# Output projection of a two-sequence encoder layer as four pairs of seven products

## The chip, the cores and the metric

The kernel runs on one core of a Trainium2 chip. The metric is device time in microseconds (us) of one execution; smaller is better. The engines are called PE (TensorE), DVE (VectorE), ACT (ScalarE), POOL (GpSimd) and SP (SyncE, which issues most transfers).

## The reference, cut to what matters

The reference is one layer of an encoder over two sequences of 512 tokens and 1024 channels: an S5 scan, a differential attention and a cross attention over a memory, whose outputs are gated, projected up and added into `merged`; then an output projection, and a feed-forward network. All is float32.

```python
merged = None
for n in range(N_BRANCH):
    term = jax.nn.sigmoid(g[..., n * D_MODEL:(n + 1) * D_MODEL]) * (branches[n] @ p['w_up'][l, n])
    merged = term if merged is None else merged + term
x = x + merged @ p['w_out'][l]
xn2 = _rmsnorm(x, p['norm_ffn'][l])
gate, up = jnp.split(xn2 @ p['w_ffn_in'][l], 2, axis=-1)
return x + (jax.nn.silu(gate) * up) @ p['w_ffn_out'][l]
```

The change is at `merged @ p['w_out'][l]`: 1024 tokens (both sequences) by 1024 channels by 1024 channels.

## The kernel before

**Matmuls.** Activations lie with channels on the 128 partitions and the tokens of both sequences (2 x 512) along the free axis, in 8 tiles of 128 channels. Every float32 operand is split into a high and a low part (`split`, L134 and L135: ACT writes the high part as float32r, DVE subtracts it from the source for the low part), and each product is three matmuls of 128 x 128 by 128 x 512: high by high, high by low, low by high (`mm3`).

**Seven products.** The feed-forward network already multiplies 2 x 2 blocks with seven products instead of eight. The two blocks of tokens are the two sequences, the two blocks of K are channel tiles i and i + 4, and the two blocks of output channels are two tiles. `quad_sums` makes four sums and differences of a pair of activation tiles, `quad_split` splits the seven operands into a pair of slots `th` and `tl` (seven columns of 512 each), `weights4` makes the seven weight operands `A11`, `A12`, `A22`, `S1` to `S4` of two weight tiles (four sums by POOL, L1022 to L1025), and `quadrants` (L1101) adds the seven results into four blocks. `products` gives the order of the matmuls.

**The stages here.** `merge_units(1, ...)` is the last merge: eight units of 24 matmuls; DVE scales each result by the gate (L789), POOL adds it into `mg[m]` (L793), and then `split` makes `mgh[m]`, `mgl[m]`. The output projection follows: `out_tile(m, s, w)` issues, for output tile m and sequence s, 8 K steps of three matmuls; DVE adds the residual x (L960) into `x1[m]`, SP stores it to `x1D` in DRAM, and ACT and POOL collect the sum of squares for the norm (`sum_sq`, L181 and L182). The order of the tiles is 0, 4, 1, 5, 2, 6 and then 3 and 7 sequence by sequence. `operands(i)` scales `x1[i]` and `x1[i + 4]` by `norm_ffn` and makes the operands of the feed-forward network from them. Then the feed-forward loop runs 22 blocks of 84 matmuls (`products(i, w)`); the first, i = 0, takes its K steps so that the operands of pairs 2 and 3 are wanted last. The norm's factor is applied to the results, so only `rstd(accs[s])` in block 0 has to wait for the sums of squares.

**What sets the order.** The framework's scheduler orders the instructions of each engine at build time, by the order of the program where they are ready, and puts the semaphores in. A pool with n buffers hands them out in turn; a new tile waits until all accesses to the one n before it are done. `issue_after` puts instructions behind a given one of their engine, and `InOrder`, with `on` set, keeps one engine to the order of the program; before the change only PE has one. The rooms that matter: `wf`, `wh`, `wl` (weights, two buffers each), `ld` (four), `x1` (four), `th0`, `tl0`, `th1`, `tl1` (two each), six PSUM banks `mm` and two `tr` (`aux`).

Of the kernel before, what the change touches and what calls it, by code (L numbers as in the profile page):

```python
# [10 lines left out]
F32 = mybir.dt.float32  # L11
# [8 lines left out]
P = 128  # L20
# [33 lines left out]
class InOrder:  # L54
# [10 lines left out]
    def matmul(self, *args, **kw):  # L65
        return self.put(self.eng.matmul(*args, **kw))  # L66

    def transpose(self, *args, **kw):
        return self.put(self.eng.transpose(*args, **kw))  # L69
# [3 lines left out]
def encoder(ctx: ExitStack, tc: tile.TileContext, a, out):  # L73
    nc = tc.nc
    V, S, PO, PE = nc.vector, nc.scalar, nc.gpsimd, InOrder(tc, nc.tensor)
# [55 lines left out]
    def split(hi, lo, src, scale=None):  # L131

        if scale is None:
            h = S.copy(hi, src)  # L134
            l_ = V.tensor_tensor(out=lo, in0=src, in1=hi.bitcast(F32), op=ALU.subtract)  # L135
# [380 lines left out]
    with behind():  # L516

        mrs = cst.tile([P, 4], F32, name="mrs")
        mbc = cst.tile([P, L], F32, name="mbc")
# [249 lines left out]
    mgh, mgl = [None] * KD, [None] * KD  # L769

    def merge_in(n, tags="yyyy"):
        bh_ = [slot(tags[t], [P, NT], F32R, f"yh{t}") for t in range(4)]
        bl_ = [slot(tags[t], [P, NT], F32R, f"yl{t}") for t in range(4)]
# [6 lines left out]
    def merge_units(n, b, m, first=False, last=False):  # L780
# [11 lines left out]
        if not first:  # L792
            PO.tensor_tensor(out=mg[m], in0=mg[m], in1=gt, op=ALU.add)  # L793
# [5 lines left out]
    mes = ExitStack()  # L799
    b0 = []  # L800

    def first_in():
        b0.append(merge_in(0, ["qk", "qk", "qk", "v"]))
        yield 0

    def merges():
        res_.close()
        xp_es.close()
        open_tags(mes, side="right", mg=8, y=8)
# [119 lines left out]
    open_tags(phase, ms=16)  # L929
    ves = ExitStack()  # L930
    open_tags(ves, z=6)
    b1 = merge_in(1, "zzzy")
    for m in range(KD):
        for _ in merge_units(1, b1, m, last=True):
            pass

    mes.close()
    ves.close()
    tes = ExitStack()
    open_tags(tes, side="right", th0=2, tl0=2)
    aes = ExitStack()
    aps = aes.enter_context(tc.tile_pool(name="ffs", bufs=1, side="right", reuse_waits="tile"))
    ses = ExitStack()
    open_tags(ses, side="right", x1=4, xr=2, ts=1)
    x1D = drp.tile([KD, P, NT], F32, name="x1D")
    x1 = {}  # L950
    accs = [new_acc() for _ in range(NS)]

    def out_tile(m, s, w):
        cs = slice(s * L, (s + 1) * L)
        xr = slot("xr", [P, L], name="xr")
        nc.sync.dma_start(xr, a["xT"][s, :, m, :])
        ps = bank()
        for k in range(KD):
            mm3([ps], w[0], w[1], [(mgh[k][:, cs], mgl[k][:, cs])], k, KD)
        V.tensor_tensor(out=x1[m][:, cs], in0=ps, in1=xr, op=ALU.add)  # L960
        nc.sync.dma_start(x1D[m, :, cs], x1[m][:, cs])
        sum_sq(accs[s], x1[m][:, cs], m == 0)

    last_p = None

    def quad_sums(xa_, xb_, tag="ts", third=PO):
# [5 lines left out]
        last_p = third.tensor_tensor(out=t_[:, 2], in0=b22, in1=b12, op=ALU.subtract)  # L972
        V.tensor_tensor(out=t_[:, 1], in0=b22, in1=t_[:, 0], op=ALU.subtract)
        V.tensor_tensor(out=t_[:, 3], in0=b21, in1=t_[:, 1], op=ALU.subtract)
        return t_

    def quad_room(i):
        j = i // 2 % 2
        return slot(f"th{j}", [P, 7, L], F32R, "th"), slot(f"tl{j}", [P, 7, L], F32R, "tl")

    last_q = None

    def quad_split(i, xa_, xb_, t_):

        nonlocal last_q
# [3 lines left out]
        split(th[:, 3:5], tl[:, 3:5], t_[:, 0:2])  # L989
        last_q = split(th[:, 5:7], tl[:, 5:7], t_[:, 2:4])  # L990
        return th, tl

    def operands(i):

        xa_, xb_ = x1[i], x1[i + 4]
        S.activation(out=xa_, in_=xa_, func=AF.Copy, scale=vcol("norm_ffn", i))
        V.tensor_scalar_mul(xb_, xb_, vcol("norm_ffn", i + 4))
        return quad_split(i, xa_, xb_, quad_sums(xa_, xb_))

    H = 4 * P  # L1000

    def weights4(i):

        nonlocal last_w
        a1, a2 = (wp.tile([P, DM], F32, tag="wf", name="wf") for _ in range(2))
        nc.sync.dma_start(a1, a["w_fg"][i])
        last_w = nc.sync.dma_start(a2, a["w_fu"][i])
        res = {}

        def sp(pool, src, sfx, *names):  # L1010
            n = len(names) * H
            nonlocal last_s
            wh, wl = (pool.tile([P, DM], F32R, tag=t_ + sfx, name=t_, bufs=2) for t_ in ("wh", "wl"))
            last_s = split(wh[:, :n], wl[:, :n], src)
# [3 lines left out]
        sp(wp, a1, "", "A11", "A12")  # L1018
        sp(wp, a2[:, H:], "", "A22")
        yield res  # L1020
# [771 lines left out]
```

## Time and profile before

| | us |
|---|---|
| three runs, median | 1604.06 |
| three runs, lowest and highest | 1603.86, 1604.61 |
| profiled execution, span from first to last instruction | 1603.0 |
| PE busy in it | 1587.1 |
| DVE, ACT, POOL busy | 1162.9, 640.0, 541.6 |

The page gives no other time of the profiled execution than its span. Its mean granted clock is 0.997 of full speed. Lines of the profile name a source line (L66), an engine, an operation and the tiles written and read (`bkmm<-th,wh`: a PSUM bank from operands `th` and weights `wh`); a releaser is what ended an engine's wait. All PE instructions are recorded by a helper and have its lines (L66 matmul, L69 transpose), so they are told apart by their tiles. A matmul's own row is longer than the distance to the next one, since matmuls are pipelined.

### The profile page before, as it was taken

What the parts mean: (1) busy time and instruction counts of PE and PEld (TensorE: products, weight loads), DVE (VectorE), ACT (ScalarE), POOL (GpSimd) and SP (SyncE); (2) the same over time, 40 slices, a digit from 0 to 9 for tenths busy, and PEclk for the clock granted to TensorE, in tenths of its full rate; (3) what the DMA queues carried; (4) which work ended last, traced back from release to release, by engine and by line L of the source; (5) the groups of instructions that cost most, each with busy time, mean ns of one, the idle gap of its engine ahead of it and who ended that gap; (6) DMA issues with size and microseconds to landing.
All of it is one profiled execution on the core that took longest, in us unless ns stands there. A gap on an engine that the chain in (4) does not pass through costs nothing.

```text
span 1603.0 us, 21625 instructions
## 1 busy us (share of the span) xinstructions
PE 1587.1 (99%) x7838; PEld 1314.8 (82%) x7838; DVE 1162.9 (73%) x1856; ACT 640.0 (40%) x1142; POOL 541.6 (34%) x449
## 2 busy tenths in 40 slices
PE   9999999999999999999999999999999999999997
PEld 7888788888898778778878878888888888788877
DVE  7976996076773766776465678888898778988654
ACT  6544323274652455574133443332333323233323
POOL 0010100001333220300343367676665553444653
PEclk9999999999999999999999999999999999999998
DMA  9554523576762111244454432333323223986222
GB/s 366 173 160 150 179 95 125 180 273 201 252 224 102 54 47 40 73 156 140 145 190 132 144 118 80 131 119 129 121 106 118 79 88 119 344 332 198 80 66 106
DMA packets 104891, 237.86 MB, mean 148 GB/s; under 512 B 13520, under 2 KB 45008, under 8 KB 104784
## 3 DMA queue, kind: packets, MB, share of 16 engines
q1 hardware_dynamic: 104784, 236.47, 43.1%
q8 instruction: 62, 1.02, 0.3%
q14 instruction: 45, 0.37, 0.1%
HBM read 165.16 MB, written 71.27 MB: 147 GB/s over the span
## 4 chain that ended last, share of the span: by engine, by line
PE 87%; issue 4%; DVE 3%; DMA 3%; POOL 2%; ACT 0%; SPq 0%; POOLq 0%; DVEq 0%; ACTq 0%
PE bkmm L66 75%; PE bksc L66 3%; PE bktr L66 2%; PE bkoo L66 2%; PE bktr L69 2%; DVE tl L135 1%; PE bktr L1626 1%; POOL mg L793 1%; PE bktr L1597 1%; DMA yt<-bD 1%; PE bktr L1686 0%; PE bktr L1687 0%; PE bktr L1685 0%; PE bktr L1565 0%; DMA acc<-in_w_fo 0%
## 5 line engine op out<-in xcount | busy, mean ns | idle before, releaser
L66 PE MATMUL bkmm<-xh,wh 128*128 128x512 f32 x640 | 255.4, 399 | 0.0
L66 PE MATMUL bkmm<-xh,wl 128*128 128x512 f32 x640 | 250.9, 392 | 0.0
L66 PE MATMUL bkmm<-xl,wh 128*128 128x512 f32 x640 | 250.5, 391 | 0.0
L66 PE MATMUL bkmm<-tl,wh 128*128 128x512 f32 (+1 forms) x621 | 241.2, 388 | 1.4 <-DVE tl L135 1.4
L66 PE MATMUL bkmm<-th,wl 128*128 128x512 f32 (+1 forms) x621 | 241.0, 389 | 0.9 <-DVE wl L135 0.9
L66 PE MATMUL bkmm<-th,wh 128*128 128x512 f32 (+1 forms) x621 | 241.1, 389 | 0.0
L134 ACT CAST wh<-wf 128x1024 fp32r<-128x1024 f32 (+1 forms) x134 | 117.9, 880 | 224.1 <-PE bkmm L66 179.8
L135 DVE TENSOR_TENSOR wl<-wf,wh 128x1024 fp32r<-128x1024 f32 (+1 forms) x134 | 145.1, 1083 | 50.2 <-ACT wh L134 45.7
L66 PEld LDWEIGHTS bkmm<-xh,wh 128*128 128x128 f32 x640 | 120.3, 188 | 30.3 <-issue 7.9
L66 PE MATMUL bkmm<-th,w 128*128 128x512 f32 x432 | 141.5, 392 | 2.7 <-DVE up L1101 1.0
L66 PEld LDWEIGHTS bkmm<-xh,wl 128*128 128x128 f32 x640 | 120.2, 188 | 26.7 <-issue 1.3
L66 PEld LDWEIGHTS bkmm<-xl,wh 128*128 128x128 f32 x640 | 120.4, 188 | 22.4 <-issue 0.4
L66 PEld LDWEIGHTS bkmm<-tl,wh 128*128 128x128 f32 x621 | 116.6, 188 | 25.9 <-DVE tl L135 2.1
L66 PEld LDWEIGHTS bkmm<-th,wl 128*128 128x128 f32 x621 | 116.5, 188 | 25.7 <-DVE wl L135 1.7
L66 PEld LDWEIGHTS bkmm<-th,wh 128*128 128x128 f32 x621 | 116.6, 188 | 23.9
L1165 POOL TENSOR_TENSOR up<-up,acc 128x512 f32<-128x512 f32 x44 | 83.6, 1920 | 87.8 <-DVE up L1101 87.8
L454 POOL TENSOR_TENSOR raw<-raw 128x128 f32<-128x128 f32 x28 | 15.2, 545 | 284.4 <-DVE nb L545 206.5
L66 PEld LDWEIGHTS bkmm<-th,w 128*128 128x128 f32 x432 | 80.9, 188 | 23.8 <-DVE up L1101 3.4
L793 POOL TENSOR_TENSOR mg<-mg,gl 128x1024 f32<-128x1024 f32 x16 | 43.5, 2720 | 139.0 <-DVE gl L789 139.0
L548 ACT ACTIVATE e<-bksc,nb 128x512 f32<-128x512 f32 (+1 forms) x96 | 58.8, 615 | 73.5 <-DVE nb L543 51.9
L66 PE MATMUL bkmm<-tl,w 128*128 128x512 f32 x216 | 84.2, 390 | 0.0
L66 PE MATMUL bkmm<-yh,wh 128*128 128x512 f32 x192 | 75.9, 397 | 0.8 <-ACT wh L134 0.4
(641 smaller groups left out, 3527.8 us busy)
## 6 DMA issues: line engine op xcount, KB each, us to landing
wf<-in_w_in SPq DMA_DIRECT2D x40, 512.0 KB, 3.9
wD<-hl SPq DMA_DIRECT2D x28, 512.0 KB, 2.9
w<-wD SPq DMA_DIRECT2D x28, 512.0 KB, 5.0
gD<-gt SPq DMA_DIRECT2D x24, 512.0 KB, 2.8
gl<-gD SPq DMA_DIRECT2D x24, 512.0 KB, 3.4
wf<-in_w_fg SPq DMA_DIRECT2D x22, 512.0 KB, 3.7
wf<-in_w_fu SPq DMA_DIRECT2D x22, 512.0 KB, 3.6
aD<-ac SPq DMA_DIRECT2D x22, 512.0 KB, 3.1
```

What stands on the lines that cost most here:

```text
L66: return self.put(self.eng.matmul(*args, **kw))
L69: return self.put(self.eng.transpose(*args, **kw))
L134: h = S.copy(hi, src)
L135: l_ = V.tensor_tensor(out=lo, in0=src, in1=hi.bitcast(F32), op=ALU.subtract)
L454: PO.tensor_tensor(out=a22, in0=a21, in1=a22, op=ALU.add)
L548: last_x = S.activation(out=e, in_=sc, func=AF.Exp, bias=nb, scale=scale, accum_out=sm)
L793: PO.tensor_tensor(out=mg[m], in0=mg[m], in1=gt, op=ALU.add)
L1165: PO.tensor_tensor(out=up, in0=up, in1=accs[s], op=ALU.mult)
L1597: PE.matmul(kp[64 * hf : 64 * hf + 48, g * 144 : (g + 1) * 144], l_[:, 2 * hf + g, :], o_[:, 4 * g4 + 2 * hf + g, :], start=(l_ is lr48), ...
L1626: PE.matmul(ps[:, g * P : (g + 1) * P], w_[:, gg * P : (gg + 1) * P], u_[:, 8 * o + gg, :], start=True, stop=True)
```

## The change

The output projection takes the form of the feed-forward network. `mg[i]` and `mg[i + 4]` become the operands `mo[i]` of seven products (`quad_steps`, which makes the four differences in place, all on DVE), and output tiles m and m + 4 are made as a pair: `out_first` (pair 0, K step by K step over seven PSUM banks), `out_pair` (pairs 1 to 3, product by product in two or three banks that are read between products and written on; in pair 3 the last three products go K step by K step). The results are added into tiles that already hold x.

`split_by_transfer` is a second way to split: ACT writes the high part and then its negative as the low part, and a transfer issued by POOL adds the source to it. It is used for the second half of the operands `mo[0]` to `mo[2]` and of pairs 0 and 2 of the feed-forward network, for `A11`, `A12` and `A22` of all pairs, for `S1` to `S4` of pairs 1 to 3, and for all but `A22` of the feed-forward network's first block.

PE is kept in program order from pair 0 to the end of block 0, DVE, ACT and POOL from `early` to the end of the stage. `early`, called in the middle of pair 3, prepares block 0's weights and the operands of pairs 1 (read back from `x1D`) and 2; the four last additions of pair 3 stand behind it. Block 0 takes its products in a new order and all its matmuls come before those of `rstd`. Rooms: `th1`, `tl1` three, `th0`, `tl0` and `th2`, `tl2` one each, `sw` (two, for `S1` to `S4`, two inputs of the merge and later two tiles of the output). The columns of `th` and `tl` have another order, and `SEVEN` with them.

```diff
-    V, S, PO, PE = nc.vector, nc.scalar, nc.gpsimd, InOrder(tc, nc.tensor)
+    V, S, PO, PE = (InOrder(tc, e_) for e_ in (nc.vector, nc.scalar, nc.gpsimd, nc.tensor))
...
+    def split_by_transfer(hi, lo, src):
+        S.copy(hi, src)
+        n_ = S.activation(out=lo, in_=src, func=AF.Copy, scale=-1.0)
+        return n_, PO.dma_start(lo.bitcast(F32), src, accum_op=ALU.add)
...
-        if last:
-            mgh[m] = slot("ms", [P, NT], F32R, f"mgh{m}")
-            mgl[m] = slot("ms", [P, NT], F32R, f"mgl{m}")
-            split(mgh[m], mgl[m], mg[m])
...
+    def quad_steps(th, tl, xa_, xb_, far=False):
...
+        split(th[:, 0], tl[:, 0], b11)
+        split(flat(th[:, 1:3]), flat(tl[:, 1:3]), xb_)
+        V.tensor_tensor(out=b11, in0=b12, in1=b11, op=ALU.subtract)
+        last_p = V.tensor_tensor(out=b12, in0=b22, in1=b12, op=ALU.subtract)
+        V.tensor_tensor(out=b22, in0=b22, in1=b11, op=ALU.subtract)
+        V.tensor_tensor(out=b21, in0=b21, in1=b22, op=ALU.subtract)
+        yield th, tl
+        put = split_by_transfer if far else split
+        put(flat(th[:, 3:5]), flat(tl[:, 3:5]), xa_)
+        last_q = put(flat(th[:, 5:7]), flat(tl[:, 5:7]), xb_)
...
-    def out_tile(m, s, w):
...
-        for k in range(KD):
-            mm3([ps], w[0], w[1], [(mgh[k][:, cs], mgl[k][:, cs])], k, KD)
-        V.tensor_tensor(out=x1[m][:, cs], in0=ps, in1=xr, op=ALU.add)
...
+    SEVEN = (("A11", 0), ("S2", 6), ("A12", 1), ("S3", 4), ("S1", 3), ("A22", 5), ("S4", 2))
...
+    for i in range(4):
         for m in (i, i + 4):
...
+            for _ in merge_units(1, b1, m, third=V if m == KD - 1 else PO):
+                pass
+        if i < 3:
+            mo.append(quad_in_place(*room_of(1), mg[i], mg[i + 4], far=True))
...
+    mo.append(quad_in_place(*room_of(2), mg[3], mg[7]))
...
+    def out_first(m, w):
...
+        for j, k in ((0, 0), (0, 1), (1, 0), (1, 1), (0, 2), (1, 2), (0, 3), (1, 3)):
+            for nm, o in SEVEN:
+                if nm[0] == "AS"[j]:
+                    product(ps[nm], w[nm], o, mo, (k,))
...
+    def out_pair(m, w):
+        xa_, xb_ = x_in(m)
+        pu, pw, pv = bank(), bank(), bank()
+        product(pu, w["A11"], 0, mo)
+        product(pv, w["A12"], 1, mo)
+        plus(xa_[:, :L], pu)
+        plus(xa_[:, :L], pv)
+        product(pu, w["S2"], 6, mo, more=True)
+        product(pw, w["S1"], 3, mo)
+        plus(xa_[:, L:], pu)
+        if m < 3:
...
+        else:
+            plus(xa_[:, L:], pw)
+            plus(xb_[:, L:], pw)
+            p4, pl = bank(), bank()
+            for k in range(4):
+                product(pu, w["S3"], 4, mo, (k,), more=True)
+                product(p4, w["S4"], 2, mo, (k,))
+                product(pl, w["A22"], 5, mo, (k,))
+            w0.append(early())
+            plus(xb_[:, :L], pu)
+            plus(xb_[:, L:], pu)
+            plus(xa_[:, L:], p4)
+            plus(xb_[:, :L], pl)
...
+    def early():
+        for e_ in (V, S, PO):
+            e_.on = True
+        wg = weights4(a["w_fg"][0], a["w_fu"][0], ("A11", "S1", "S3"), True)
+        w_ = next(wg)
+        x2_ = [slot("ld", name="xo") for _ in range(2)]
+        for t_, r_ in zip((1, 5), x2_):
+            nc.sync.dma_start(r_, x1D[t_])
+        scaled_x(1, *x2_)
+        scaled_x(2, *xs_[2])
+        next(wg)
+        next(wg)
+        ops.append(quad_in_place(*quad_room(1), *x2_))
+        g = quad_steps(*quad_room(2), *xs_[2], far=True)
+        ops.append(next(g))
+        next(wg)
+        next(g, None)
+        return w_
...
+    for m in range(4):
+        w = all_of(weights4(a["w_out"][m], a["w_out"][m + 4], FAR if m else FAR[:2]))
+        xs_.append((out_pair if m else out_first)(m, w))
+        if m == 0:
+            ops.append(quad_in_place(*quad_room(0), *scaled_x(0, *xs_[0]), far=True))
+    ops.append(quad_in_place(*quad_room(3), *scaled_x(3, *xs_[3], *(slot("ld", name="xs") for _ in range(2)))))
+    x_sums(3, *xs_[3])
...
         if i == 0:
...
+            ps = [bank() for _ in range(6)] + [aux()]
+            ps = [ps[j] for j in (0, 2, 3, 4, 6, 1, 5)]
+            near_, far_ = ("A11", "S2", "A12", "S1"), ("A22", "S3", "S4")
+            for k, names in ((0, near_), (1, near_), (0, far_), (1, far_), (2, near_ + far_), (3, ("A11", "A12", "A22")),
+                             (3, ("S2", "S3", "S1", "S4"))):
+                for nm in names:
+                    j = [n_ for n_, _ in SEVEN].index(nm)
+                    product(ps[j], w[nm], SEVEN[j][1], ops, (k,))
```

In `weights4`, a split whose first name is in `moved` goes by `split_by_transfer`; `FAR` is `("A11", "A22", "S1", "S3")`.

More of the change, by code (lines that the diff above doesn't have):

```diff
@@ L993, in operands, with flat, room_of @@
[L993 to L998, printed above, removed]
+    open_tags(ves, z=1)
+    x1D = drp.tile([KD, P, NT], F32, name="x1D")
+    accs = [new_acc() for _ in range(NS)]
+    def flat(t_):
+        return t_.rearrange("p a n -> p (a n)")
+    def room_of(j):
+        return slot(f"th{j}", [P, 7, L], F32R, "th"), slot(f"tl{j}", [P, 7, L], F32R, "tl")
@@ new lines, in product @@
+    def product(ps, w, o, ops_, ks=range(4), more=False):
+        nonlocal last_mm
+        wh, wl = w
+        mark = {"skip_group_check": True} if more else {}
+        for k in ks:
+            th, tl = ops_[k]
+            ws_ = slice(k * P, (k + 1) * P)
+            PE.matmul(ps, wh[:, ws_], th[:, o], start=(k == 0 and not more), stop=False, **mark)
+            PE.matmul(ps, wh[:, ws_], tl[:, o], start=False, stop=False, **mark)
+            last_mm = PE.matmul(ps, wl[:, ws_], th[:, o], start=False, stop=(k == 3), **mark)
```

256 lines of the change are left out of this document (143 added, 113 removed).

## The prediction

> **What bounds the kernel now.** I read the page's table of engines first, then the chain of waits, then the stages around the change, then single rows.
>
> ```profile
> PE 1587.1 (99%) x7838; PEld 1314.8 (82%) x7838; DVE 1162.9 (73%) x1856; ACT 640.0 (40%) x1142; POOL 541.6 (34%) x449
> ...
> PE 87%; issue 4%; DVE 3%; DMA 3%; POOL 2%; ACT 0%; SPq 0%; POOLq 0%; DVEq 0%; ACTq 0%
> ```
>
> TensorE (PE) is busy all the time and carries the chain; the other engines only matter where they make it wait. The next rows are the stages of busy time (last merge; output projection; the start of the feed-forward loop, "FFN 0" below), one piece of the chain, and the two places in FFN 0 where PE stands.
>
> ```profile
> 812.00:855.20 43.20, 43.20 (x192) 35.74 (x192) 27.18 (x32) 11.62 (x14) 20.49 (x8) 1.00 0.48 164
> 855.20:942.40 87.20, 87.20 (x386) 72.23 (x385) 47.44 (x48) 33.46 (x39) 35.08 (x22) 1.00 0.49 148
> 942.40:965.00 22.60, 21.22 (x102) 17.15 (x101) 22.32 (x21) 13.92 (x19) 16.03 (x13) 1.00 0.32 97
> ...
> 811.79 130.82 PE bkmm L66 x576
> ...
> 957.88 0.49 PE L66 MATMUL bkmm<-th,wh 128*128 128x512 f32 x1
> 958.98 0.50 PE L66 MATMUL bkmm<-tl,wh 128*128 128x512 f32 x1 [0.60 <-DVE tl L135]
> ...
> 960.02 0.40 PE L66 MATMUL bkmm<-th,wl 128*128 128x512 f32 x1
> 961.20 0.50 PE L66 MATMUL bkmm<-tl,wh 128*128 128x512 f32 x1 [0.78 <-DVE tl L135]
> ```
>
> The columns after the window are its length, then PE, PEld, DVE (VectorE), ACT (ScalarE), POOL (GpSimd), the granted clock, the DMA share and GB/s. The clock is 1.00 throughout. The chain runs through merge and output projection as 576 matmuls without a hole in 130.82 us: one costs 130.82 / 576 = 0.227 us, not the 0.39 us of its own row, since matmuls overlap. FFN 0 starts without a gap and then stands twice: 958.98 - 957.88 - 0.227 = 0.87 us and 961.20 - 960.02 - 0.227 = 0.95 us, together 1.8 us, for low parts (`tl`) from VectorE. So time is won here only by issuing fewer matmuls, and lost wherever an operand comes later than PE's order wants it.
>
> **What it removes.** The output projection now issues 8 tiles x 2 sequences x 8 K steps x 3 = 384 matmuls; four pairs of seven products of 4 K steps x 3 are 336. 48 x 0.227 = 10.9 us of path. FFN 0 still has 84. The 1.8 us of standing in FFN 0 I count as removed and price that boundary afresh: the ceiling is 12.7 us.
>
> **What it adds**, in the rows that price it:
>
> ```profile
> L134 ACT CAST wh<-wf 128x1024 fp32r<-128x1024 f32 x8 | 8.4, 1054 | 17.8 <-PE bkmm L66 17.8
> L134 ACT CAST wh<-wf 128x512 fp32r<-128x512 f32 x1 | 0.6, 626 | 1.3 <-PE bkmm L66 1.3
> L996 ACT ACTIVATE x<-x,vec 128x1024 f32<-128x1024 f32 x4 | 4.6, 1154 | 8.1 <-DMA x1D<-x 8.1
> ...
> L135 DVE TENSOR_TENSOR wl<-ws,wh 128x1024 fp32r<-128x1024 f32 x2 | 2.5, 1226 | 6.4 <-ACT wh L134 6.4
> L971 DVE TENSOR_TENSOR ts<-x 128x512 f32<-128x512 f32 x3 | 2.1, 693 | 9.3 <-ACT x L996 9.3
> L960 DVE TENSOR_TENSOR x<-bkmm,xr 128x512 f32<-128x512 f32 x16 | 10.9, 684 | 17.3 <-PE bkmm L66 17.3
> L1022 POOL TENSOR_TENSOR ws<-wf 128x512 f32<-128x512 f32 x1 | 1.3, 1297 | 1.0 <-DMA wf<-in_w_fu 1.0
> ...
> aD<-ac SPq DMA_DIRECT2D x22, 512.0 KB, 3.1
> ...
> fb<-aD SPq DMA_DIRECT2D x9, 512.0 KB, 6.2
> ...
> x1D<-x SPq DMA_DIRECT2D x16, 256.0 KB, 2.4
> ```
>
> No row of before shows an accumulating transfer, nor any DMA that POOL issues. A plain 512 KB store out of SBUF lands in 3.1 us and a 256 KB one in 2.4 us; the slowest 512 KB row quoted is 6.2 us, and a POOL sum of 1.3 us can stand ahead of the issue. So a low part made this way comes 2.4 to 7.5 us after ScalarE's second pass, instead of 1.23 us after its first. I take 3.1 and 2.4, the rows nearest in kind (the source is SBUF, the queues about half empty at a DMA share of 0.49). Below nothing I do not go: a transfer that waits for a pass of ScalarE cannot land before it.
>
> [...]
>
> Steady state is covered. A pair is 84 x 0.227 = 19.1 us. Per pair ScalarE makes eight weight passes (six of 1.05 us, two of 0.63 us) and four squares, under 11 us; VectorE adds seven or eight results, 8 x 0.68 = 5.5 us; POOL does four sums and four additions to the squares, 8 x 1.3 = 10.4 us, and four issues. Room for `A11` comes free after 24 of 84 matmuls, so the next split has 60 x 0.227 = 13.6 us. In one PSUM bank reused by three products each reading has 12 matmuls, 2.7 us, for 0.68 us. SyncE's queue gets eight 512 KB loads of x for sixteen of 256 KB, eight stores for sixteen, and two loads back of pair 1: nothing at that DMA share. Three places are not covered: where one stage's weights or operands hand their room to the next.
>
> *Merge to pair 0.* `A22` takes the room of the last merge unit's weights, free 0.39 - 0.23 = 0.16 us after the merge. Two passes of 0.63 us and 2.4 us of transfer: 3.8 us. PE wants the low part as its ninth matmul, at 8 x 0.227 = 1.8 us. Cost 2.0 us. This hides `mo[3]`, whose last part is wanted only after 63 matmuls, 14.3 us.
>
> *Pair 0 to pair 1.* Pair 0 runs K by K, so the room of `A11`, `A12` comes free at its 69th matmul: 16 x 0.227 - 0.39 = 3.2 us before pair 1. Two passes of 1.05 us and 3.1 us: 2.0 us after the start; wanted at the third matmul, 0.45 us. Cost 1.5 us.
>
> *Pair 3 to FFN 0.* Count from the first FFN 0 matmul. VectorE, ScalarE and POOL are put in program order here, and `early()` stands ahead of pair 3's own last four additions, so those wait for it, and PE for them. ScalarE may begin when the room of `A11` is free, 61 x 0.227 - 0.39 = 13.5 us before. Two passes (2.1), four scalings (4.6) and two passes (2.1) bring it to -4.7. The operands of pair 1 may be made: `mo[0]` was free at -6.0, which is what the K order of the last pair is for. High part 0.63, low part 0.69: -3.4; the next high part is ready, and on VectorE follow 1.23, four differences 2.8 and two low parts 2.5: 3.3. Pair 1's last column is wanted at 15 matmuls, 3.4 us: just covered. Then pair 2's first half (0.69 + 1.23 + 2.8) and `A22` (0.69): 8.7; two additions from `pu`: 10.1. Instructions of VectorE follow one another closer than their rows:
>
> ```profile
> 936.07 1.23 DVE L135 TENSOR_TENSOR wl<-ws,wh 128x1024 fp32r<-128x1024 f32 x1 [1.67 <-ACT wh L134]
> 937.22 0.69 DVE L960 TENSOR_TENSOR x<-bkmm,xr 128x512 f32<-128x512 f32 x1
> ```
>
> by 0.08 us, so 14 of them take 1.1 us less: 9.0. PE wants that bank after 24 matmuls, 5.4 us: it stands 3.6 us. Pair 3's operands come after the additions: two scalings, high parts, then 1.23 + 2.8 + 2.5 us on VectorE, ending near 20.3, for a column wanted 45 matmuls after the bank, 9.0 + 10.2 = 19.2, plus one for the low part: 1.0 us more. Cost 4.6 us. The two norm factors (`rstd`) go from the middle of FFN 0 to its end; the matmuls of the next block are free of the fixed order and cover them.
>
> The sum: -12.7 + 2.0 + 1.5 + 4.6 = -4.6 us. The profiled span of 1603.0 us becomes 1598.4 us. The median of the runs, 1604.06 us, is 1.1 us above that span, so I forecast **1599.5 us**.
>
> **The rivals.** *The transfers land late (slower).* Place: the low parts of `A22`, `A11` and of pair 2's differences. At 7 us instead of 3.1 us (6.2 us and something ahead of it on POOL) the first two boundaries lose 3.9 us each; pair 2's last part, whose second pass ends at 10.9, lands at 17.9 for a want at 9.0 + 18 x 0.227 + 0.9 = 14.0, and 3.9 us minus the 1.0 us it absorbs are lost: 10.7 us more, 1610 us. It decides from about 5 us: there the two boundaries lose 3.8 and pair 2 0.9, and the gain is gone. For it: nothing of this kind has been seen here, and loads under load take 6.2 us. Against it: plain stores in the same stage are at 2.4 us.
>
> *VectorE becomes the bound in the last merge.* The differences of three pairs move into a stage where POOL adds too.
>
> ```profile
> L793 POOL TENSOR_TENSOR mg<-mg,gl 128x1024 f32<-128x1024 f32 x15 | 41.1, 2742 | 42.7 <-DVE gl L789 42.7
> ...
> L135 DVE TENSOR_TENSOR mgl<-mg,mgh 128x1024 fp32r<-128x1024 f32 x8 | 12.9, 1619 | 11.7 <-ACT mgh L134 11.7
> ...
> 947.95 1.78 DVE L135 TENSOR_TENSOR tl<-x,th 128x512 fp32r<-128x512 f32 x1
> ...
> 952.68 2.32 DVE L135 TENSOR_TENSOR tl<-x,th 128x1024 fp32r<-128x1024 f32 x1
> ```
>
> An addition of two SBUF operands takes 0.69 us alone and 1.78 us beside POOL; of 1024 columns 1.23 and 2.32. VectorE was busy 27.2 of 43.2 us here, 12.9 of them `mgl`, which goes. Three pairs' work is 3 x (0.69 + 1.23 + 4 x 0.69) = 14.0 us alone, 28.3 in all, which fits; wholly beside POOL it is 3 x (1.78 + 2.32 + 4 x 1.78) = 33.7, 48.0 in all, 4.8 us too much, and pair 0's two low parts that VectorE still makes come 2.2 us later: 7.0 us, 1606.5 us. It decides where a pair's work passes (43.2 - 14.3) / 3 = 9.6 us. The POOL additions fill 7 x 2.7 us = 19 us of the 43.2, so half overlap is likelier, and that fits. [...]
>
> *All covers hold.* The transfers land within 2 us and the scheduler finds `early()` earlier; about 1.5 us of stalls are left: 1593 us. Against it stands the fixed order on VectorE, which is counted out above.
>
> That matmuls do not fall by 48 I exclude: the loops give the count.
>
> **How the numbers follow.** This kernel can be told from no change at about 0.2%, 3.2 us. My forecast has a chance of 0.42 (its own range 1596 to 1603.5, of which 0.30 is more than 3.2 us under the median and 0.12 within it); late transfers 0.26 (0.24 slower, 0.02 within); VectorE 0.20 (0.14 slower, 0.06 within); covers hold 0.12. Faster 0.42, same 0.20, slower 0.38. Both signs hold much of the chance, so the range goes from just above the best case, 1594, to the late transfers, 1611.
>
> **What would show it.** PE matmuls down by 48 to 7790. In the groups, PE's idle time put down to a DMA or `wl` near the ninth matmul of pair 0 and the third of pair 1 (about 2.0 and 1.5 us), and to the additions of pair 3 in FFN 0 (about 3.6 us). The DMA table should show the accumulating transfers with their time to land: 3 us confirms, over 5 us is the first rival. VectorE's mean for the differences in the merge tells the second: near 0.7 us or near 1.8 us, and whether weights of merge units come late. I am wrong if PE stands more than 12.7 us longer than before between the merge and the end of FFN 0, or if stages away from it change by more than 1 us.

## The result, and the profile after

The changed kernel takes 1653.71 us in the median of four runs (1650.86 to 1655.55), the kernel before 1604.09 on the same chip: a ratio of 1.0309, 95% interval 1.0296 to 1.0321. It is 49.6 us slower, far beyond the forecast of 1599.5 us and its range. The profiled execution has a span of 1652.6 us (1603.0 before) and a mean granted clock of 0.982 (0.997).

The first two parts of the page of the changed kernel (engines; shares of the chain):

```profile
PE 1593.2 (96%) x7790; PEld 1315.0 (80%) x7790; DVE 1172.5 (71%) x1876; ACT 676.3 (41%) x1188; POOL 578.3 (35%) x491
...
PE 82%; DMA 5%; issue 5%; DVE 4%; POOL 2%; ACT 1%; SPq 0%; POOLq 0%; ACTq 0%; DVEq 0%
```

PE issues 48 matmuls fewer, as said, and yet is busy 6 us longer over a span 50 us longer: it stands, and part of its matmuls are slower. DMA has risen from 3% to 5% of the chain. The stages (window, length, then PE, PEld, DVE, ACT, POOL busy, the granted clock, DMA share, GB/s) are the last merge; pair 0; pairs 1 and 2 with the first third of pair 3, in two parts; and most of FFN 0, which starts at 982.15 us:

```profile
812.88:860.50 47.62, 46.10 (x192) 36.77 (x192) 39.69 (x42) 20.15 (x25) 23.51 (x12) 0.96 0.69 193
860.50:898.30 37.80, 22.94 (x85) 17.77 (x85) 20.27 (x19) 13.53 (x18) 18.63 (x15) 0.77 0.51 132
898.30:945.00 46.70, 34.91 (x136) 27.59 (x135) 13.87 (x20) 25.02 (x31) 26.69 (x25) 0.89 0.85 213
945.00:967.00 22.00, 14.82 (x64) 11.97 (x63) 4.03 (x6) 10.77 (x14) 12.15 (x11) 0.88 0.79 237
...
986.00:1016.00 30.00, 23.33 (x83) 17.99 (x83) 22.21 (x24) 17.95 (x23) 16.39 (x12) 0.83 0.48 124
```

Pair 0 takes 37.8 us for its 84 matmuls (19.1 us at the pitch of before). The DMA share is 0.79 to 0.85 in the middle of the output projection, where it was 0.49. And the granted clock, 1.00 in all these stages before, is 0.77 to 0.96. What PE waited for between 855 and 1010 us (sum, times, longest):

```profile
PE bkmm L67 <- DMA wl<-wf: 18.1, 3, 12.9
PE bkmm L67 <- DMA sw<-ws: 11.5, 4, 7.2
PE bkmm L67 <- DVE x L67: 8.3, 2, 7.5
PE bkmm L67 <- DMA tl<-x: 5.2, 1, 5.2
```

Three of these four are the accumulating transfers. The table of transfers between 812 and 1010 us (queues: packets, MB, share of the time of 16 engines; then issues: KB each, median us to landing):

```profile
q0 software_dynamic: 3888, 13.11, 35.5%
q1 hardware_dynamic: 7776, 22.02, 31.8%
...
wf<-in_w_out SPq DMA_DIRECT2D x8, 512.0 KB, 5.5
...
sw<-ws POOLq DMA_DIRECT2D x8, 512.0 KB, 8.1
x1D<-x SPq DMA_DIRECT2D x8, 512.0 KB, 8.9
tl<-mg POOLq DMA_DIRECT2D x6, 512.0 KB, 6.0
wl<-wf POOLq DMA_DIRECT2D x5, 512.0 KB, 6.0
tl<-x POOLq DMA_DIRECT2D x4, 512.0 KB, 6.9
...
wl<-wf POOLq DMA_DIRECT2D x4, 256.0 KB, 7.5
```

A low part lands 6.0 to 8.1 us after its issue, not 3.1. The transfers of POOL (q0) move 13.11 MB and take more engine time than 22.02 MB of all the others. Ordinary traffic pays too: the stores of x land in 8.9 us, in the kernel before in 2.4 us for half the size (and in 2.7 us for the same size in e5 below, which has no transfers of POOL).

The first stand on PE's timeline, at the start of pair 0:

```profile
860.99 0.40 PE L67 MATMUL bkmm<-tl,wh 128*128 128x512 f32 x1
874.24 0.79 PE L67 MATMUL bkmm<-th,wl 128*128 128x512 f32 x1 [12.85 <-DMA wl<-wf]
874.83 0.63 PE L67 MATMUL bkmm<-th,wh 128*128 128x512 f32 x1
875.26 0.63 PE L67 MATMUL bkmm<-tl,wh 128*128 128x512 f32 x1
```

PE stands 13 us for the low part of `A11`, and the matmuls behind it start 0.43 us apart instead of 0.227. POOL's timeline says why the transfer was so late:

```profile
859.48 3.29 POOL L67 TENSOR_TENSOR ws<-wf 128x512 f32<-128x512 f32 x2 [4.23 <-DMA wf<-in_w_out]
...
863.96 3.32 POOL L67 TENSOR_TENSOR mg<-mg,gl 128x1024 f32<-128x1024 f32 x1
...
867.81 1.19 POOL L67 DMA_DIRECT2D wl<-wf  x1
...
872.03 0.87 POOL L67 DMA_DIRECT2D wl<-wf  x1 [0.92 <-ACT sw L67]
884.61 1.29 POOL L67 TENSOR_TENSOR ws<-wf 128x512 f32<-128x512 f32 x1 [11.71 <-DMA wf<-in_w_out]
```

The issue (867.81) stood in POOL's queue behind sums that waited for the second weight tile and behind an addition of the merge, though ScalarE had ended its second pass for `A11` at 861.55; 6.4 us after the issue it landed. The last row shows the return: POOL then waits 11.7 us for the next weights. The longest pieces of DMA on the chain of waits from 780 to 1030 us (start, length) show that circle:

```profile
872.03 7.09 DMA wl<-wf
...
904.17 10.56 DMA x1D<-x
...
935.76 10.06 DMA wl<-wf
945.83 5.77 DMA wf<-in_w_out
...
961.81 7.99 DMA wl<-wf
...
993.86 10.36 DMA tl<-x
```

The accumulating `wl<-wf` of 935.76 reads `wf`, so that room is not free until 945.8; only then the next weights load, POOL sums them (951.7 to 956.8), and their low parts go by transfer again (issued at 957.90): PE stands 7.3 us for `sw`. `x1D<-x` at 904.17 is a plain store: the scaling of x in place waits for it, VectorE's queue for the operand made of that, and pair 1's additions stand behind it for 7.6 us.

**A ledger.** From PE's timeline between the start of the last merge and the end of the stands in FFN 0 I summed the idle times that have a named releaser (the bracket of a row; "waits") and, apart from them, all other time beyond 0.227 us from one matmul to the next ("slow"). The length of a single stand in the text is the distance beyond 0.227 us, some 0.2 us more than the named idle time. Before (811.7 to 965 us): 1.4 us of waits and 1.05 us of the rest. After (812.8 to 1012): 44.4 us of waits and 19.4 us of matmuls that merely come slowly. 44.4 + 19.4 - 2.45 - 10.9 (the 48 matmuls) = 50.4 us, and the span grew by 49.6. So two questions: what makes the waits, and what makes the slow matmuls.

### The profile page after: what moved, and what is told of

It is laid out like the page before. It is cut to its first block, busy times and chain, and to the rows that moved or that the text cites. A ratio compares the mean times of both kernels' runs of the same rounds, so it can differ in the third digit from the quotient of the medians.

```text
span 1652.6 us, 21684 instructions
## 1 busy us (share of the span) xinstructions
PE 1593.2 (96%) x7790; PEld 1315.0 (80%) x7790; DVE 1172.5 (71%) x1876; ACT 676.3 (41%) x1188; POOL 578.3 (35%) x491
## 3 DMA queue, kind: packets, MB, share of 16 engines
q0 software_dynamic: 3888, 13.11, 4.3%
## 4 chain that ended last, share of the span: by engine, by line
PE 82%; DMA 5%; issue 5%; DVE 4%; POOL 2%; ACT 1%; SPq 0%; POOLq 0%; ACTq 0%; DVEq 0%
PE bkmm L67 70%; PE bktr L67 5%; PE bksc L67 2%; PE bkoo L67 2%; DMA wl<-wf 2%; DVE tl L67 1%; PE bktr L1762 1%; POOL mg L67 1%; POOL ws L67 1%; DMA x1D<-x 1%; DMA tl<-x 1%; DVE ts L67 1%; DVE mg L67 1%; DMA fb<-aD 1%; PE bktr L1733 1%
## 5 line engine op out<-in xcount | busy, mean ns | idle before, releaser
L67 PE MATMUL bkmm<-th,sw 128*128 128x512 f32 x808 | 268.1, 396 | 19.0 <-DMA sw<-ws 11.5
L67 PEld LDWEIGHTS bkmm<-th,sw 128*128 128x128 f32 x808 | 154.2, 191 | 53.5 <-DMA sw<-ws 13.2
L67 PE MATMUL bkmm<-tl,sw 128*128 128x512 f32 x404 | 159.4, 394 | 5.2 <-DMA tl<-x 5.2
L67 POOL TENSOR_TENSOR raw<-raw 128x128 f32<-128x128 f32 x112 | 60.7, 547 | 290.4 <-DVE nb L67 206.5
L67 PE MATMUL bkmm<-th,wl 128*128 128x512 f32 (+1 forms) x321 | 127.7, 398 | 19.0 <-DMA wl<-wf 18.1
L67 PE MATMUL bkmm<-th,wh 128*128 128x512 f32 (+1 forms) x321 | 127.1, 396 | 0.8 <-DVE x L67 0.8
L67 PE MATMUL bkmm<-tl,wh 128*128 128x512 f32 (+1 forms) x321 | 126.8, 395 | 0.0
L67 POOL TENSOR_TENSOR ws<-wf 128x512 f32<-128x512 f32 x52 | 87.4, 1700 | 86.1 <-DMA wf<-in_w_fu 58.5
L67 PEld LDWEIGHTS bkmm<-tl,sw 128*128 128x128 f32 x404 | 77.3, 191 | 21.9 <-DMA tl<-x 5.6
L67 ACT CAST sw<-ws 128x1024 fp32r<-128x1024 f32 x52 | 54.4, 1047 | 89.6 <-PE bkmm L67 59.8
```

The lines of the kernel that those rows point to most:

```text
L67: return lambda *args, **kw: self.put(f(*args, **kw))
```

## The experiments

All times are medians (the kernel before, run beside each group, took 1603.89 to 1604.35 us); waits and slow matmuls are this ledger, between 812 and 985 us (for the changed kernel to 1012). In the slowest versions FFN 0 goes on behind 985 us: in e4 a wait of 4.6 us for additions of pair 3 is left out, in e9 one of 3.8 us for `tl`.

| kernel | us | ratio to before, 95% | waits | slow |
|---|---|---|---|---|
| changed | 1653.71 | 1.0296–1.0321 | 44.4 | 19.4 |
| e1: low parts by VectorE | 1624.18 | 1.0114–1.0144 | 21.7 | 9.9 |
| e2: plain copies | 1633.06 | 1.0168–1.0198 | 27.4 | 12.3 |
| e3: only operands by transfer | 1629.4 | 1.0146–1.0176 | 23.4 | 12.5 |
| e4: only weights by transfer | 1643.4 | 1.023–1.0264 | 32.1 | 10.1 |
| e5: e1, merge additions on VectorE | 1615.82 | 1.0062–1.0092 | 17.1 | 7.2 |
| e6: e1, pair 3's additions first | 1631.71 | 1.0158–1.0189 | 25.1 | 12.1 |
| e7: e1, pair 0's weights first | 1622.64 | 1.01–1.0134 | 21.6 | 9.2 |
| e8: e5, e6, e7 together | 1623.07 | 1.0106–1.014 | 18.5 | 12.7 |
| e9: changed, merge additions on VectorE | 1640.87 | 1.0216–1.0246 | 30.3 | 14.1 |
| e10: e5 and 5 transfers in `early()` | 1617.5 | 1.0067–1.0097 | 18.5 | 8.4 |
| e11: e5 and 13 transfers, none for the projection's weights | 1619.4 | 1.0076–1.0118 | 21.0 | 8.3 |
| e12: e5 and 6 transfers, the merge's | 1611.07 | 1.0029–1.0063 | 13.6 | 4.6 |
| e15: e12, additions between | 1617.83 | 1.0062–1.0096 | 14.2 | 9.5 |
| e16: e12, another bank order | 1611.45 | 1.003–1.006 | 13.4 | 7.6 |

**The transfers.** My theory after the result was the first rival: the accumulating transfers land late and hold the rooms behind them. The other theory: the seven products are late by themselves, VectorE above all.

e1, all low parts made by VectorE again:

```diff
 def split_by_transfer(hi, lo, src):
-    S.copy(hi, src)
-    n_ = S.activation(out=lo, in_=src, func=AF.Copy, scale=-1.0)
-    return n_, PO.dma_start(lo.bitcast(F32), src, accum_op=ALU.add)
+    return split(hi, lo, src)
```

> Every split goes by ScalarE and VectorE again; nothing else is changed. Theory A (the accumulating transfers land in 6 to 8 us, fill the DMA engines, and hold rooms so long that loads, sums and PE come late): PE's named waits between the last merge and the end of the first feed-forward block fall from 44 us to under 15 us, and the time to 1600-1612 us. Theory B (the seven products with fixed orders on four engines and VectorE's extra work are what stands, whichever way the low parts are made): 1630 us or more.

It takes 1624.18 us: the 27 transfers cost 29.5 us, and 20 us of loss remain without any.

e2, the same transfers, but plain (it leaves the addition out):

```diff
-    return n_, PO.dma_start(lo.bitcast(F32), src, accum_op=ALU.add)
+    return n_, PO.dma_start(lo.bitcast(F32), src)
```

> The 27 transfers stay where they are, issued by POOL, but copy the source over the low part instead of adding to it, so the low parts hold wrong values and only the time is read. Theory A1 (the addition is what is slow): they land in 3 to 4 us, the DMA share of the stage falls, and the time comes to 1605-1620 us. Theory A2 (any transfer issued by POOL in this place is slow, or the rooms' chains are): landing stays over 5 us and the time over 1635 us.

Its transfers in the same stretch:

```profile
q0 software_dynamic: 3632, 13.11, 16.8%
...
sw<-ws POOLq DMA_DIRECT2D x8, 512.0 KB, 6.5
tl<-mg POOLq DMA_DIRECT2D x6, 512.0 KB, 3.3
wl<-wf POOLq DMA_DIRECT2D x5, 512.0 KB, 3.1
tl<-x POOLq DMA_DIRECT2D x4, 512.0 KB, 4.1
...
wl<-wf POOLq DMA_DIRECT2D x4, 256.0 KB, 4.3
```

The same bytes from the same queue take 16.8% of the engines' time instead of 35.5%, and every group lands sooner, by 1.6 us (`sw`) to 3.2 us (`wl` of 256 KB). So the addition itself, not POOL's issuing, doubles the time of the transfer engines; it is worth 1653.71 - 1633.06 = 20.6 us of the 29.5. It is not all of the landing: `sw` still takes 6.5 us as a plain copy.

e3 and e4, one half of the transfers each:

```diff
# e3, in weights4
-                split_by_transfer(wh[:, :n], wl[:, :n], src)
+                last_s = split(wh[:, :n], wl[:, :n], src)
# e4, in quad_steps
-        put = split_by_transfer if far else split
+        put = split
```

> The weights' low parts are made by VectorE, the differences of the operands still by 10 accumulating transfers. Theory A with the weights as the main place (wl was waited for 18.1 us, sw 11.5 us, tl 5.2 us): 1608-1620 us. If the operands' transfers are as bad: 1630 us or more. Theory B: no better than 1640 us.

> The reverse: the differences of the operands by VectorE, the weights' 17 accumulating transfers stay. Theory A with the weights as the main place: 1635-1650 us. If the operands were as bad: under 1630 us.

Without the 17 transfers of weights 24.3 us come back, without the 10 of operands 10.3. Weights are the greater part: their transfers hold `wf`, on which the next load and POOL's sums wait.

**VectorE in the merge, and the order.** e1 leaves pair 0's weights 9.7 us late. Theory: VectorE's subtractions are slowed by POOL's additions of the merge (the second rival). Rivals: the order in the program, of pair 3's additions and of pair 0's weights.

```diff
# e5 (with e1's edit)
-            for _ in merge_units(1, b1, m, third=V if m == KD - 1 else PO):
+            for _ in merge_units(1, b1, m, third=V):
# e6 (with e1's edit): out_pair, m == 3
-            w0.append(early())
             plus(xb_[:, :L], pu)
...
             plus(xb_[:, :L], pl)
+            w0.append(early())
# e7 (with e1's edit): ahead of mo.append(quad_in_place(*room_of(2), mg[3], mg[7]))
+    w_first = all_of(weights4(a["w_out"][0], a["w_out"][4], ("A11", "A22")))
```

> As e1 (no transfers), with the additions into mg on VectorE in all eight merge units, not in the last alone. Theory C (what is left at the start of pair 0 comes from POOL's 1024-column additions, beside which VectorE's two-SBUF-operand instructions of 0.7 us take 2.9 us): the waits for wl at the start of pair 0 fall from 9.7 us to under 4 us and the time from 1624 to 1615-1619 us. Theory D (VectorE simply has too much to do there; 7 more additions of 1.2 us make it worse): 1626 us or more.

> As e1, with pair 3's four last additions put ahead of early(). Theory E (the fixed order is what makes the first feed-forward block stand 6.7 us at its far products): that wait falls under 2 us, and since the operands of pairs 1 to 3 then come some 2.8 us later, 2 to 5 us of it are won: 1619-1622 us. If VectorE is saturated there in any order, the time goes to other operands: 1623-1626 us.

> As e1, with pair 0's weights ahead of the operands of mo[3] in the program. Theory F (the order is what makes the weights late, since mo[3] is wanted only 14 us after pair 0 begins): waits for wl at pair 0 fall by half, 1617-1620 us. Theories C and D: within 2 us of 1624 us.

> The edits of e5, e6 and e7 together on e1. If C, E and F each hold: 1604-1610 us, near before. If VectorE is saturated: 1620 us or more.

e5 wins 8.4 us, and the waits for `wl` at pair 0 fall from 9.7 to 0.6 us. The groups of VectorE between 815 and 875 us (count, busy, mean ns), of the changed kernel, of e1 and of e5:

```profile
L67 DVE TENSOR_TENSOR wl<-wf,wh 128x512 fp32r<-128x512 f32 x7 | 11.5, 1638 | 0.2 <-ACT wh L67 0.2
```

```profile
L67 DVE TENSOR_TENSOR wl<-wf,wh 128x512 fp32r<-128x512 f32 x7 | 9.2, 1309 | 0.0
```

```profile
L67 DVE TENSOR_TENSOR wl<-wf,wh 128x512 fp32r<-128x512 f32 x7 | 4.8, 684 | 0.0
```

The same subtraction takes 1.64, 1.31 and 0.68 us. In e1 five of the seven take 0.68 or 0.69 us, and the two others begin while POOL adds:

```profile
845.28 2.87 DVE L67 TENSOR_TENSOR wl<-wf,wh 128x512 fp32r<-128x512 f32 x1
...
844.31 3.30 POOL L67 TENSOR_TENSOR mg<-mg,gl 128x1024 f32<-128x1024 f32 x1 [1.40 <-DVE gl L67]
```

VectorE has more additions to do in e5 and is done earlier. e6 is slower than e1 by 7.5 us: the 6.7 us for pair 3's additions are gone, but the weights and operands behind them are waited for instead (3.1 us for `wl`, beside the same 9.7 at pair 0 as in e1, and 5.8 for `th` and `tl`), and 2.2 us more of slow matmuls are counted. e7 changes neither wait. e8 is worse than e5 alone. The order was not it.

e9 makes the same edit in the changed kernel, with all its transfers:

> The changed kernel with all its transfers, and the additions into mg on VectorE in all units. If POOL's additions and the transfers cost independently, 8 us are won as from e1 to e5: about 1645 us. If the first stall is the transfers' alone (A11's low part queues behind them on POOL and in the DMA engines): over 1650 us.

1640.87 us: 12.8 us of the 49.6 hang on POOL's additions in the merge, partly through VectorE and partly through POOL's queue (the stand for `A11` falls from 13.0 to 6.8 us).

**Which transfers pay.** From e5, three choices of what goes by transfer: only those in `early()` (e10), all but the projection's weights (e11), only the merge's six (e12).

> As e5, with accumulating transfers only in early(): A11, S1, S3 of the first feed-forward block and pair 2's differences (5 of 27). They take 5.8 us off VectorE, which is busy without a gap there. With few others in flight they should land in 5 to 6 us. If VectorE's work is the price of that boundary (6.7 us of standing in e1 and e5), 2 to 4 us are won: 1612-1614 us. If the landing is the price, nothing or a loss: 1616-1622 us.

> As e5, with all transfers except those of the output projection's weights (13 of 27). If only the weights' transfers cost, as e3 against the changed kernel says (24 of 29 us): 1607-1614 us. If operand transfers delay x1D's stores and loads as well: 1617-1623 us.

> As e5, with accumulating transfers only for mo[0] to mo[2] (6 of 27), which are wanted late, so that their landing of 6 us is covered. They take 6.9 us off VectorE in the last merge, where it is busy 42.8 of 46.2 us. If that work is what makes pair 0's S operands late (3.4 us of waits for sw, 1.5 for ScalarE), 2 to 5 us are won: 1611-1614 us; if the transfers delay the weights' loads, a loss.

Against e5 e10 is 1.7 us slower and e11 3.6, both within overlapping intervals; the merge's six alone are 4.7 us faster (the intervals just touch, but every run of e12 is below every run of e5), since nothing wants them for long: their landing of 5.7 us is hidden. No other transfer of POOL runs in that kernel, so close to 6 us are what an accumulating 512 KB took in that stage even then. From e11 to e9 the projection's 14 weight transfers alone cost 21.5 us. e12, at 1611.07 us, is with e16 the best of all versions and still slower than before.

**What is left in e12.** PE's longest wait is the one at pair 3 to FFN 0 that the forecast, with some of VectorE's work there given to transfers, put at 3.6 us. Its row on PE's timeline, and the windows of the stand and behind it:

```profile
952.83 0.76 PE L67 MATMUL bkmm<-th,wh 128*128 128x512 f32 x1 [6.72 <-DVE x L67]
```

```profile
945.00:953.00 8.00, 1.28 (x6) 0.77 (x6) 7.90 (x11) 2.09 (x2) 1.35 (x2) 0.76 0.21 66
953.00:956.00 3.00, 3.00 (x8) 2.32 (x9) 0.88 (x2) 2.62 (x4) 2.92 (x3) 0.50 0.64 261
```

VectorE is busy 7.90 of 8.00 us while PE is busy 1.28. Is it its order, or the amount? e15 puts the four additions (`put`), `A22`, `S3` and `S4` between pair 1's operands and pair 2's. e16 gives each bank of pairs 1 and 2 24 matmuls between two uses instead of 12 (5 us of waits there):

```diff
# e15, in early()
         ops.append(quad_in_place(*quad_room(1), *x2_))
+        put()
+        next(wg)
         g = quad_steps(*quad_room(2), *xs_[2])
         ops.append(next(g))
-        next(wg)
# e16, out_pair, m < 3: A11, A12, S1, S2, A22, S4, S3
+            product(pw, w["S1"], 3, mo)
+            plus(xb_[:, L:], pw)
+            product(pu, w["S2"], 6, mo, more=True)
+            plus(xa_[:, L:], pu)
+            product(pv, w["A22"], 5, mo)
+            plus(xb_[:, :L], pv)
...
```

> The kernel with transfers only in the merge and VectorE's merge additions, with pair 3's four additions, then A22 and S3, S4 of the first feed-forward block, put between pair 1's operands and pair 2's on VectorE (they stood behind pair 2's). There VectorE worked without a gap from 932.6 to 953.9 us and PE stood 6.7 us for the additions at its end. If the order makes the stand: the four additions end near 945, PE stands under 1 us there, and 1 to 3 us for pair 2's last columns and pair 3's first, so 2 to 5 us are won. If the amount of VectorE's work makes it: the stand moves to pair 2's or pair 3's low parts and the time stays within 1.5 us of 1611.1.

> The kernel with transfers only in the merge and VectorE's merge additions, with another order of products in pairs 1 and 2: A11, A12, S1, S2, A22 (in a bank of its own), S4, S3, so that each bank has 24 matmuls between two uses and not 12; it costs one VectorE addition more in each of the two pairs. PE stood there 2.2, 0.3, 2.1 and 0.4 us for results that VectorE had not read yet. If 12 matmuls (2.7 us) of cover are too few: these 5 us go, and with them about 1 us of slow matmuls, near 1605. If VectorE is behind by more than 24 matmuls: the stands stay, within 1 us of 1611.1.

Neither helps. In e15 the wait for the additions is gone, and 2.7 us for `th` and 2.6 for `tl` stand in its place, then 2.5 for pair 3's: 14.2 us of waits for 13.6. It is 6.8 us slower than e12, which neither expectation allowed for; 4.9 us of that are more slow matmuls, and I did not look for the rest. In e16 the waits at the banks (2.2, 0.3, 2.1 and 0.4 us) become 0.2 and, in pair 2, one of 4.8 us, in a stretch (899 to 910 us) in which VectorE is busy 10.51 of 11.00 us. Both orders moved the wait to what they put last; I take it that VectorE has more to do there than PE leaves it time for. It has time elsewhere (19.06 of 33 us busy in e12 from 899 to 932), so another spread of its work, pair 0's operands put off for instance, may still win; it wasn't tried.

**The slow matmuls.** Theory A: a stand of PE itself makes what follows slow. Theory B: the transfers or VectorE's load do. These four kernels are the kernel before, with passes of ScalarE that write a tile over itself, so that PE must wait in a quiet stage.

```diff
# e13: 12 passes behind sequence 0 of tile 1; e14: 3 each for tiles 4, 1, 5, 2
                 out_tile(m, s, w)
+                for _ in range((12 if m == 1 else 0) if s == 0 else 0):
+                    S.copy(w[1], w[1].bitcast(F32))
# e18: 14 passes; e19: 8
+                for _ in range(14 if (m, s) == (1, 0) else 0):
+                    S.copy(mgl[7], mgl[7].bitcast(F32))
```

> The kernel before with one stand of PE put in by hand: between the two sequences of output tile 1, ScalarE writes the tile's low weights over themselves twelve times (nothing changes in them), and PE's next matmuls need them. Twelve passes of about 1.05 us are 12.6 us, less the two matmuls that can still go (0.45 us): a stand of about 12.5 us. In the changed kernel the time beyond the named waits was 19.4 us for 44.4 us of waits, 0.44 us for each. Theory A (a stand itself makes the matmuls behind it come slower and the granted clock fall): the time grows by the stand and by 3 to 6 us more, matmuls behind it come about 0.42 us apart, and the granted clock of that stage is below 1. Theory B (the slow spells of the changed kernel come from its transfers or from VectorE's load): the time grows by the stand alone, 12 to 13 us, and matmuls behind it are 0.227 us apart.

> The kernel before with four short stands: the same twelve passes of ScalarE, three each in output tiles 4, 1, 5 and 2, so about 3 us of standing at a time, 12 us in all. Theory A with a spell of fixed length behind every stand: four spells, so more than in the kernel with one stand, 8 us or more beyond the stands. Theory A with a spell in proportion to the stand: about the same 3 to 6 us as there. Theory A with a threshold: short stands cost themselves alone. Theory B: stands alone, 12 us.

> The kernel before with one stand of PE that no other matmul can fill: behind sequence 0 of output tile 1, ScalarE writes the last K tile's low part (mgl[7]) over itself fourteen times (nothing changes in it), and all output tiles after it need that part at their eighth K step. Fourteen passes at 0.96 us are 13.4 us; seven K steps (4.8 us) go on beside them: PE stands about 8.5 us in a stage with no transfer of POOL and little VectorE work. If a stand by itself slows what is behind it: the granted clock behind the stand is 0.5, matmuls are 0.43 us apart for some 6 to 10 us, and the time grows by 8.5 us and 3 to 5 more. If the slow spells need the load of the feed-forward boundary: 8.5 us alone, clock 1.00.

> The same with eight passes: 7.7 us, less the 4.8 us that go on, a stand of about 2.9 us. In the kernel with four groups of passes 1.8 us of standing within 3.3 us left the clock at 1.00, in the one with twelve passes 2.2 us alone did, and 3.1 us within 6 us halved it. If the stand decides by its length: either 2.9 us alone, or 2.9 us and 3 to 5 us of slow matmuls; the row of the clock says which.

The scheduler filled most of the stands with matmuls of other tiles, so the sizes expected were all missed: e13 1612.1 us (ratio 1.0036 to 1.0066), e14 1605.21 (1.0001 to 1.0019), e18 1607.1 (1.0012 to 1.0031), e19 1604.24 (0.9994 to 1.0013). But two of them answer the question. e18 has one stand in the output projection, with no transfer of POOL; VectorE is idle until it ends. PE's timeline, and the windows of the stand and behind it:

```profile
897.50 0.39 PE L66 MATMUL bkmm<-mgh,wh 128*128 128x512 f32 x1
900.06 0.50 PE L66 MATMUL bkmm<-mgl,wh 128*128 128x512 f32 x1 [2.17 <-ACT mgl L1039]
...
901.33 0.63 PE L66 MATMUL bkmm<-mgl,wh 128*128 128x512 f32 x1
901.76 0.63 PE L66 MATMUL bkmm<-mgh,wl 128*128 128x512 f32 x1
```

```profile
896.00:900.00 4.00, 1.89 (x9) 1.24 (x7) 0.00 (x0) 3.90 (x4) 0.00 (x0) 1.00 0.01 2
900.00:904.00 4.00, 3.94 (x11) 3.08 (x12) 3.12 (x4) 3.06 (x5) 0.28 (x1) 0.60 0.38 106
```

A stand of 2.3 us, and behind it matmuls 0.43 us apart and a clock of 0.60 for 4 us. Theory A holds: no accumulating transfer is needed. Behind the stand VectorE is busy again (3.12 of 4.00 us), but its load alone does not do it: in FFN 0 of the kernel before it is busy 22.32 of 22.60 us at a clock of 1.00, and behind e12's stand 0.88 of 3.00 at 0.50. e13 shows that it is not the length of the stand alone. Its stand at 894 us, behind which the clock stays at 1.00, is nearly as long (2.2 us); in FFN 0 stands of 0.8 and 1.4 us within 4 us, with 0.3 us more of named idle right behind, brought the clock to 0.5 for most of 10 us:

```profile
894.18 0.39 PE L66 MATMUL bkmm<-mgh,wl 128*128 128x512 f32 x1
896.65 0.50 PE L66 MATMUL bkmm<-mgh,wh 128*128 128x512 f32 x1 [2.08 <-ACT wh L134]
```

```profile
897.00:899.00 2.00, 1.93 (x9) 1.28 (x8) 0.85 (x1) 1.94 (x3) 0.00 (x0) 1.00 0.66 143
...
966.00:969.00 3.00, 3.00 (x10) 2.08 (x8) 3.00 (x4) 1.99 (x3) 3.00 (x3) 0.50 0.30 87
```

Stands of 0.9 and 1.0 us within 4 us, as the kernel before and e14 have them there, leave it at 1.00. So much these runs show: behind some stands the granted clock falls to 0.50 (e12, e13) and the matmuls come 0.427 us apart for 0.227; one stand of 2.3 us was enough for a slow spell (e18), and a few short ones (e13), while one of 2.2 us (e13) and two of 0.9 and 1.0 us (before) were not. What decides between them no run shows.

## Why the prediction was wrong

**The matmuls.** Right: 7790, 10.9 us of path. It is the only term that came out as worked.

**The landing.** Mis-sized: "I take 3.1 and 2.4, the rows nearest in kind" was 6.0 to 8.1 us for 512 KB and 7.5 for 256 KB. For plain transfers of POOL 3.1 is right in two of e2's four groups of 512 KB (4.1 and 6.5 us in the others); I knew no row of an addition and took the near end of the bounds 2.4 to 7.5, where the rows could not tell. The quicker groups of e2, issued by POOL, are at 3.1 and 3.3 us near SyncE's 512 KB store of before (3.1).

**"Steady state is covered".** The step that failed worst. I counted the engines' passes and the bytes ("nothing at that DMA share"), but not that a transfer holds its source. VectorE's 128x1024 subtraction frees `wf` after 1.2 us (e5); the transfer frees it after 6 to 10 (6.0 in the median, 10.06 at 935.76), and load, sums and the next split shift with it. Nor that the additions take the transfer engines twice as long for the same bytes (35.5% against e2's 16.8% of their time for 13.11 MB), and that SyncE's stores and loads land later beside POOL's transfers: `x1D<-x` in 8.9 us, in e2 in 6.9, in e5 without any in 2.7; the projection's weights in 5.5, 4.0 and 3.5 us. 7.6 us of PE's wait at 915.7 (a store) and 7.3 at 958.5 (POOL's sums) lie inside what I called covered; with the bank reuse, called covered by 12 matmuls, as much as 5 us more in e12.

**Merge to pair 0: 2.0 us.** It was 13.0 and 2.4. I followed `A22`; the wait was `A11`, and the cause POOL's queue, in which its issue stood behind sums waiting for a load and behind a merge addition. I had let at most one POOL sum of 1.3 us stand ahead of an issue; here 6.3 us passed between ScalarE's pass and the issue. The 2.4 us for `A22` come on top of the 13.0; that they lie near the 2.0 written is chance.

**Pair 0 to pair 1: 1.5 us.** 3.4 us, by the landing: ScalarE's passes ended 1.4 us before the pair, about as written (1.1), but the low part came 5.2 us behind them, where 3.1 stood.

**Pair 3 to FFN 0: 4.6 us.** 9.2 us of named waits in the changed kernel: 5.2 for `tl<-x`, 3.2 for `sw`, and only 0.8 for the additions behind `early()`, to which the forecast gave 3.6. e10, which keeps the transfers of this boundary and no others, waits 5.3, 0.8 and 2.1 us for the same three. So the wait for the additions is there, but smaller than written, and the transfers, which land in 8.9 us (`tl`) in e10 and were taken as covered, cost more than it. e12's 6.7 us for the additions is no test of the 3.6, since VectorE makes these low parts itself there. The working also has a slip of 0.2 us: -3.4 + 1.23 + 2.8 + 2.5 is 3.1, not 3.3.

**First rival.** Its mechanism was right, and its point of decision (5 us) passed; its price of 10.7 us above the forecast is a third of the 29.5 that e1 measured, since it counted three boundaries and no rooms.

**Second rival.** Also true at the same time, which I had not allowed for: the cases were priced one instead of the other. VectorE was busy 39.69 us in the last merge, between my 28.3 and 48.0; POOL's additions there cost 8.4 us (e1 to e5), 12.8 with the transfers (e9), where 7.0 was written. The rows of 1.64, 1.31 and 0.68 us (the changed kernel, e1, e5) go the way of before's 1.78 us beside POOL and 0.69 alone.

**The clock.** Missing altogether: "the clock is 1.00 throughout" was read as a constant. Every stand was priced at its own length; 18.3 us of the loss (19.4 - 1.05) are matmuls that come slowly, where the granted clock of the stages is 0.77 to 0.96.

**My own test.** I wrote that I am wrong if PE stands over 12.7 us longer: it stood 43 us longer. The stages away from the change moved by about 1.1 us ahead of it (the merge starts at 812.88 for 811.79); I did not look into that.

What stays open: why some stands halve the clock and others of nearly the same length (2.3 us in e18, 2.2 in e13) don't was seen, not controlled; and no experiment put VectorE's work in the output projection off to where it has time, so that e12's remaining 6.7 us were only shown to move, not to go. Nor was the program order that is forced on DVE, ACT and POOL from `early` on taken away; only orders within it were changed.

## What to carry to other kernels

A transfer that replaced an engine's instruction held its source and its target until it landed (6 to 10 us here, where VectorE's subtraction took 1.2 in e5): count the rooms it keeps, not its bytes, and put it only where nothing wants source or result for some 10 us (e12's six) and where its issue doesn't stand behind waiting work. In a kernel in which PE is 99% busy, price stands at about 1.4 times their length (an estimate from this kernel, 63.8 us for 44.4; single ones cost more or nothing extra), and ask of saved matmuls first whether the engines that feed PE have room for the additions they bring. Work on the idler engine slowed the busier one here (VectorE's subtraction 1.31 us in the mean in e1, 0.68 in e5): the merge's additions on VectorE made the kernel 8.4 us faster.

## What the runs showed that I had not expected

- An accumulating transfer of 512 KB within SBUF took 6.0 to 8.1 us to land (medians of the groups of the changed kernel; 4.4 to 8.9 in e9 to e12), a plain one from the same queue 3.1 and 3.3 us in two of four groups and 4.1 and 6.5 in the others; for 13.11 MB 35.5% of the engines' time against 16.8%.
- VectorE's 128x512 subtraction of two SBUF operands took 2.87 us beside POOL's 128x1024 additions, 0.68 us without (e1).
- A stand of PE of 2.3 us was followed by matmuls 0.427 us apart and a granted clock of 0.60 over 4 us (e18); another of 2.2 us was not (e13, clock 1.00).
- The scheduler fills a stand put in by hand: of 12 and 14 passes of ScalarE PE felt 2.2 and 2.3 us.
